# A decoder trunk in float32: where the moving operands of its matmuls lie within 256 bytes, how factors share tiles, and who adds the last squares

## The chip, the cores and the metric

The kernel runs on one core of a Trainium2 chip. The metric is the device time of one execution in microseconds (us); lower is better. The core has TensorE for matmuls (PE in the profile, with its weight loads under PEld), VectorE (DVE), ScalarE (ACT), GpSimd (POOL) and the DMA queues, each with an instruction stream of its own; semaphores tie them together. SBUF is the memory that the engines read, PSUM the one that matmuls write.

## The reference, cut to what matters

```python
def rms_norm(x, g):
    y = x * lax.rsqrt(jnp.mean(x * x, axis=-1, keepdims=True) + 1e-6)
    return y * g
def swiglu(x, w_gate, w_up, w_down):
    return (jax.nn.silu(x @ w_gate) * (x @ w_up)) @ w_down
for layer in range(2):                         # x: 512 tokens x 1024
    x = x + 0.5 * swiglu(rms_norm(x, ffn1_norm), ...)     # 1024 -> 2816 -> 1024
    hn = rms_norm(x, mix_norm)
    x = x + (pool_mla_mixer(hn, ...) if layer == 0 else gated_conv_mixer(hn, ...))
    x = x + 0.5 * swiglu(rms_norm(x, ffn2_norm), ...)
```

Everything is float32. There are four feed-forward blocks, one mixer with pooling and attention, one with a short gated convolution, and six norms that are taken over the 1,024 channels of a token.

## The kernel before

Tokens lie along the free dimension: `x[k]` holds 128 channels by 512 tokens, for k from 0 to 7. A matmul keeps a 128x128 block of weights stationary and streams activations as the moving operand, 512 tokens or, in the feed-forward blocks, half of them (256 columns). To reach float32 precision each product is made of three matmuls on operands that are split in a high and a low half: `whi` with the high half of the activation, `whi` with its low half, `wlo` with its high half. `split` (L86 to L88) makes such halves: ScalarE rounds the high half, VectorE subtracts.

**Feed-forward block** (`ffn`). A 2x2 block product is done with seven multiplications in place of eight, so weights and activations are combined first. The seven combinations of the normed input are the tiles `fB11`, `fT1`, `fN2`, `fB21`, `fT3`, `fN22`, `fT4` (8,192 bytes in a partition, the high halves in the first 4,096 and the low halves behind). Eleven pairs p of hidden blocks each pass through seven gate/up products P1 to P7 (`gate_up`); a product is 24 matmuls with 256 columns, all with the one line L461. The result h of a pair is again split into seven factors (`blocks`, `pair_halves`), which the down products read (`down`): four pairs in the first group, four in the second, three in the last, so 24 or 18 matmuls to a product. In all four blocks together 6,720 gate/up and 3,696 down matmuls have 256 columns. `staggered` sets the order of the products of neighbouring units, and `weights()` the order of loads and splits. Four quarters of weights are loaded for each unit, and combinations of them are made by DMAs that add to what lies in SBUF.

Around the feed-forward blocks 1,668 matmuls of the three-fold kind have 512 columns: on the scaled input `xh`, `xl` (1,200), the convolution's `vh`, `vl` (192), the mixer's `mh`, `ml` and some of attention.

**Places of tiles.** Pools lay their tiles one behind the other in each partition, so a tile's address is settled by what stands ahead of it. Every weight half starts at 128 bytes past a multiple of 256. Read off the built programs, the start of a moving operand past a multiple of 256 bytes is:

| moving operand | columns | matmuls | before | after the change |
|---|---|---|---|---|
| `fB11` to `fT4` (gate/up) | 256 | 6,720 | 160 | 64 |
| factors of h in the pool `hy` (down) | 256 | 2,064 | 160 | 64 |
| factors of h in the pool `hx` (down) | 256 | 1,632 | 128 | 64 |
| `xh`, `xl` | 512 | 1,200 | 128 | 128 |
| `vh`, `vl` (convolution) | 512 | 192 | 0 | 128 |
| `mh`, `ml` (mixer) | 512 | 204 | 64 | 128 |
| attention, and its projections | 256 to 512 | 360 | 64 | 128 |

Before, a factor's two 256-column blocks share one 2,048-byte tile and the low halves lie in another tile of the pools `hx` or `hy`, at whatever distance these give; `slot` picks the pool by p.

**Norms.** `squares` has ScalarE square `x[k]`; GpSimd adds the squares of k = 0 to 5 into `acc` (L250), and those of 6 and 7 are kept in `Norm.late`. `norm_columns` sums over channels with small matmuls (`ones` as moving operand, two columns): 4 blocks of tokens for each of the three tiles, and as they are plain float32, two passes for each, so 24. VectorE and ScalarE make the reciprocal root, `norm_rows` spreads it over the partitions (L333), and ScalarE copies it to the tile `R` (L335), which the whole normed input waits for (`normal`). `copied` (L466) puts the sums `x1` and `x2` of P1, P7 and P6 in SBUF.

Of the kernel before, what the change touches and what calls it, by code (L numbers as in the profile page):

```python
# [10 lines left out]
F32 = mybir.dt.float32  # L11
F32R = mybir.dt.float32r
# [4 lines left out]
P = 128  # L17
D = 1024
T = 512
FF = 2816  # L20
NK = D // P
NF = FF // P
NT = T // P
# [12 lines left out]
HT = T // 2  # L36
# [5 lines left out]
def trunk(ctx: ExitStack, tc: tile.TileContext, a, out):  # L42
# [12 lines left out]
    nc = tc.nc  # L55
    const = ctx.enter_context(tc.tile_pool(name="const", bufs=1))
    xp = ctx.enter_context(tc.tile_pool(name="xp", bufs=1))
    wp = ctx.enter_context(tc.tile_pool(name="wp", bufs=3))
    hx = ctx.enter_context(tc.tile_pool(name="hx", bufs=16))
    tp = ctx.enter_context(tc.tile_pool(name="tp", bufs=2))  # L60
    sp = ctx.enter_context(tc.tile_pool(name="sp", bufs=3))
    pp = ctx.enter_context(tc.tile_pool(name="pp", bufs=6, space=bass.MemoryType.PSUM))

    def bank(tag="bank", bufs=None):
# [10 lines left out]
    ones = const.tile([P, 2], F32, name="ones")  # L75
# [10 lines left out]
    def split(raw, hi, lo):  # L86
        nc.scalar.copy(hi, raw)  # L87
        nc.vector.tensor_sub(lo, raw, hi.bitcast(F32))  # L88
# [75 lines left out]
    for l in range(2):  # L164
        for f in ("ffn1", "ffn2"):
# [21 lines left out]
            for kind, p in what:  # L187
                if kind == "gu":
                    units.append(seven([gu[p, q] for q in range(4)], CH, turn))
                else:  # L190
                    gi, e = p
# [35 lines left out]
    xs = [None] * NK  # L227

    class Norm:
        acc = None  # L230
        late = []

    def scaled(k, which):
        g = gains[:, which, k:k + 1]
        xh = hx.tile([P, T], F32R, tag="hx", name=f"xh{k}")
        xl = hx.tile([P, T], F32R, tag="hx", name=f"xl{k}")
        nc.scalar.activation(xh, x[k], AF.Copy, scale=g)
        nc.vector.scalar_tensor_tensor(xl, x[k], g, xh.bitcast(F32), ALU.mult, ALU.subtract)  # L238
        xs[k] = (xh, xl)
# [69 lines left out]
    def token_sums(ps, acc):  # L309

        for i in range(NT):
            nc.tensor.matmul(ps[:, 2 * i:2 * i + 2], acc[:, i * P:(i + 1) * P], ones,
                             start=True, stop=True)

    def norm_columns():

        ps = held()
        parts = [Norm.acc, *Norm.late]
        Norm.late.clear()
        for j, acc in enumerate(parts):  # L320
            for i in range(NT):
                nc.tensor.matmul(ps[:, 2 * i:2 * i + 2], acc[:, i * P:(i + 1) * P], ones,  # L322
                                 start=i + j == 0, stop=j == len(parts) - 1, skip_group_check=True)
        v = sp.tile([P, NT], F32, tag="nv", name="nv")
        nc.vector.tensor_scalar(v, ps[:, 0:2 * NT:2], 1.0 / D, EPS, ALU.mult, ALU.add)
        return rsqrt(v, NT, "n")
# [12 lines left out]
    def ffn(l, f, which, after, first=False):  # L339
        what, order = plans[l, f]  # L340
        with ExitStack() as es:
# [59 lines left out]
            quarter(banks[0:2], 4, False, True)  # L401
            quarter(banks[2:4], 4, False, True)

            hy = es.enter_context(tc.tile_pool(name="hy", bufs=19, reuse_waits="tile"))
            hfac = {}

            def slot(p, i, name):
                pool = (hx if i >= 5 else hy, hx, hx, hy, hy)[p % 5]
                return pool.tile([P, T], F32R, tag="hx" if pool is hx else "hy", name=name)

            def pair_halves(p, i, src):
                hi, lo = slot(p, i, "hh"), slot(p, i + 1, "hl")
                h3, l3 = (t.rearrange("p (e t) -> p e t", t=HT) for t in (hi, lo))
                split(src, h3, l3)
                return [(hi[:, e * HT:(e + 1) * HT], lo[:, e * HT:(e + 1) * HT]) for e in range(2)]

            B12, N22, B11, T1, N2, T3, B21, T4 = range(8)

            def blocks(p, hz, rest):

                d = hfac.setdefault(p, {})
                if not rest:
                    nc.vector.tensor_sub(hz[:, T1], hz[:, B12], hz[:, B11])
                    nc.vector.tensor_add(hz[:, N2], hz[:, T1], hz[:, N22])
                    nc.vector.scalar_tensor_tensor(hz[:, T3], hz[:, N22], -1.0, hz[:, B12], ALU.mult, ALU.subtract)
                    d["B11"], d["T1"] = pair_halves(p, 0, hz[:, B11:T1 + 1])
                    d["N2"], d["T3"] = pair_halves(p, 2, hz[:, N2:T3 + 1])
                    n22 = slot(p, 4, "hn")
                    split(hz[:, N22], n22[:, :HT], n22[:, HT:])
                    d["N22"] = n22[:, :HT], n22[:, HT:]  # L430
                else:
                    nc.vector.scalar_tensor_tensor(hz[:, T4], hz[:, N2], -1.0, hz[:, B21], ALU.mult, ALU.subtract)
                    d["B21"], d["T4"] = pair_halves(p, 5, hz[:, B21:T4 + 1])


            hz = eight()
# [25 lines left out]
                                         stop=last and i == 2, skip_group_check=True)  # L462

            def copied(ps, name):
                c = fp.tile([P, T], F32, tag=name, name=name)
                nc.scalar.copy(c, ps)  # L466
                return c

# [81 lines left out]
    def even_mixer(after):  # L550
        with ExitStack() as es:
            mp = es.enter_context(tc.tile_pool(name="mp", bufs=1))

            def one(shape, name, dt=F32):
                return mp.tile(shape, dt, tag=name, name=name)
# [1 line left out]
            pcol = one([P, 4], "pcol")  # L557
            lcol = one([P, 5], "lcol")
            qcol = one([DQK, 2], "qcol")
            rcnt = one([P, 16], "rcnt")  # L560
            mask = one([P, P], "mask")
            nc.scalar.dma_start(out=pcol, in_=a["a_pool_scale"])
            nc.scalar.dma_start(out=lcol, in_=a["a_lat_gain"])
# [354 lines left out]

    def odd_mixer(after):
        with tc.tile_pool(name="op", bufs=1) as op:  # L920
            cw = op.tile([P, 3, NK], F32, tag="cw", name="cw")
            nc.scalar.dma_start(out=cw, in_=a["c_conv_w"])
            vs = []
            for j in range(NK):
                gc = bank()
                column(gc, weights(), xs)
                if j == 0:
                    r = norm_columns()
                hh = bank()
                column(hh, weights(), xs)  # L930
                if j == 0:
                    R, _ = norm_rows(r)
                    R2 = op.tile([P, T], F32, tag="Rh", name="R2", bufs=1)
                    nc.vector.tensor_mul(R2, R, R)
                gb = bank()
                column(gb, weights(), xs)
                u = tp.tile([P, T], F32, tag="t", name="u")
                nc.vector.tensor_mul(u, gc, R2)
                nc.vector.tensor_mul(u, hh, u)
                y = op.tile([P, T], F32, tag="hf", name="y", bufs=2)  # L940
                nc.vector.tensor_scalar(y, u, cw[:, 2, j:j + 1], None, ALU.mult)
                for s in (1, 2):
                    nc.vector.scalar_tensor_tensor(y[:, s:], u[:, :T - s], cw[:, 2 - s, j:j + 1], y[:, s:],
                                                   ALU.mult, ALU.add)
                b = tp.tile([P, T], F32, tag="sq", name="b")
                nc.vector.tensor_mul(b, gb, R)
                nc.vector.tensor_mul(b, b, y)
                vh = op.tile([P, T], F32R, tag=f"vh{j}", name=f"vh{j}")
                vl = op.tile([P, T], F32R, tag=f"vl{j}", name=f"vl{j}")
                split(b, vh, vl)  # L950
                vs.append((vh, vl))
            for m in range(NK):
                y = bank()
                column(y, weights(), vs)
                nc.vector.tensor_add(x[m], x[m], y)
                after(m)
# [78 lines left out]
```

## Time and profile before

| | |
|---|---|
| median of 3 runs | 1809.54 us (1809.44 to 1812.14) |
| profiled execution | 1814.28 us, of which the span of instructions is 1812.5 us |
| TensorE's mean granted clock | 0.977 of 2.4 GHz |
| busy share: PE, PEld, DVE, ACT, POOL | 96%, 91%, 73%, 50%, 17% |
| idle time of PE put down to a wait, all lines | 58.7 us |
| read from HBM | 299.06 MB |

The span is what lies between the first and the last instruction; 1.78 us of the profiled time lie outside it. Matmuls are pipelined: their durations in the trace overlap, so the rate of a stream is read from the starts of its matmuls, not from the duration of one.

### The profile page before, as it was taken

Reading aid. Unit: us, or ns where it says so; the run is one execution under the profiler, and the core shown is the slowest. Engines: PE = TensorE matmul, PEld = TensorE weight load, DVE = VectorE, ACT = ScalarE, POOL = GpSimd, SP = SyncE. Lnnn points to the kernel's source line nnn. Section 1 sums busy time; section 2 is a strip of 40 time slices with the busy share of each in tenths; the row PEclk is TensorE's granted clock in tenths of the full one; section 3 lists DMA queues with packets and bytes.
Section 4 is the critical chain, followed back from the end, with each engine's and each line's share of the span. In section 5 each row is a group of like instructions: output and inputs, shape, how many; then the busy total and the mean of one; then the engine's idle time right before and its main releaser. Section 6 shows DMA issues by size and latency. Waiting matters only on the chain.

```text
span 1812.5 us, 31505 instructions
## 1 busy us (share of the span) xinstructions
PE 1749.0 (96%) x12738; PEld 1646.9 (91%) x12738; DVE 1326.1 (73%) x1903; ACT 907.7 (50%) x1324; POOL 308.8 (17%) x359
## 2 busy tenths in 40 slices
PE   8899999999999899999989999998999999999998
PEld 6899999988888899999979999998888879999998
DVE  6877786767887877786787867867555667867866
ACT  5554554554655554554555645544322346545553
POOL 2111111124202111111111111112000201111111
PEclk8899999999999899999998999999999989999999
DMA  6689988641015689988757988885322348888985
GB/s 200 152 208 211 220 204 205 149 137 35 18 48 163 153 209 209 213 210 205 150 153 174 212 219 210 204 211 121 105 93 95 103 128 186 219 209 205 211 207 127
DMA packets 89186, 303.21 MB, mean 167 GB/s; under 512 B 10704, under 2 KB 11472, under 8 KB 89040
## 3 DMA queue, kind: packets, MB, share of 16 engines
q0 software_dynamic: 36864, 130.04, 41.1%
q1 hardware_dynamic: 50512, 169.89, 26.9%
q8 instruction: 100, 1.64, 0.4%
q10 hardware_dynamic: 1664, 1.26, 0.2%
q14 instruction: 46, 0.38, 0.1%
HBM read 299.06 MB, written 2.10 MB: 166 GB/s over the span
## 4 chain that ended last, share of the span: by engine, by line
PE 86%; DVE 6%; DMA 3%; issue 2%; ACT 2%; POOL 1%; SPq 0%; ACTq 0%; DVEq 0%; POOLq 0%
PE bank L461 63%; PE bank L215 6%; PE bank L216 6%; PE bank L217 6%; DMA sto<-in_ffn_w_down 2%; DVE wlo L88 1%; DMA sto<-in_ffn_w_gu 1%; PE held L322 1%; ACT whi L87 1%; DVE x L531 1%; DVE xn L373 1%; DVE xl L238 1%; PE bank L866 0%; PE held L215 0%; PE held L216 0%
## 5 line engine op out<-in xcount | busy, mean ns | idle before, releaser
L461 PE MATMUL bank<-fT,whi 128*128 128x256 f32 x1920 | 349.9, 283 | 0.0
L87 ACT CAST whi<-sto 128x1024 fp32r<-128x1024 f32 (+1 forms) x192 | 196.7, 1024 | 288.7 <-PE bank L461 167.1
L461 PE MATMUL bank<-hh,whi 128*128 128x256 f32 x1056 | 299.6, 284 | 9.8 <-ACT whi L87 7.8
L461 PEld LDWEIGHTS bank<-fT,whi 128*128 128x128 f32 x1920 | 299.7, 192 | 0.8 <-ACT x L466 0.8
L461 PE MATMUL bank<-hl,whi 128*128 128x256 f32 x1056 | 297.2, 282 | 1.8 <-DVE hl L88 1.8
L88 DVE TENSOR_TENSOR wlo<-sto,whi 128x1024 fp32r<-128x1024 f32 (+1 forms) x192 | 228.6, 1191 | 93.6 <-ACT whi L87 93.0
L461 PE MATMUL bank<-hh,wlo 128*128 128x256 f32 x1056 | 296.7, 282 | 0.0
L461 PE MATMUL bank<-fT,wlo 128*128 128x256 f32 x960 | 273.2, 285 | 16.5 <-DVE wlo L88 16.5
L461 PE MATMUL bank<-fN,whi 128*128 128x256 f32 x1280 | 239.7, 288 | 9.1 <-ACT whi L87 8.9
L461 PE MATMUL bank<-fB,whi 128*128 128x256 f32 x1280 | 232.8, 280 | 0.0
L461 PEld LDWEIGHTS bank<-fN,whi 128*128 128x128 f32 x1280 | 201.2, 194 | 17.0 <-ACT whi L87 10.0
L461 PEld LDWEIGHTS bank<-hh,whi 128*128 128x128 f32 x1056 | 199.8, 189 | 13.9 <-ACT whi L87 10.2
L87 ACT CAST whi<-a 128x1024 fp32r<-128x1024 f32 (+1 forms) x128 | 130.9, 1023 | 155.7 <-issue 96.8
L461 PEld LDWEIGHTS bank<-hl,whi 128*128 128x128 f32 x1056 | 200.8, 190 | 2.6 <-DVE hl L88 2.6
L461 PEld LDWEIGHTS bank<-fT,wlo 128*128 128x128 f32 x960 | 184.6, 192 | 17.3 <-DVE wlo L88 17.3
L461 PEld LDWEIGHTS bank<-hh,wlo 128*128 128x128 f32 x1056 | 199.8, 189 | 0.0
L88 DVE TENSOR_TENSOR wlo<-a,whi 128x1024 fp32r<-128x1024 f32 (+1 forms) x128 | 154.9, 1210 | 60.7 <-ACT whi L87 60.6
L461 PEld LDWEIGHTS bank<-fB,whi 128*128 128x128 f32 x1280 | 197.8, 189 | 0.3
L124 POOL DMA_DIRECT2D sto<-in_ffn_w_gu x120 | 104.7, 873 | 519.2 <-DVE wlo L88 320.4
L88 DVE TENSOR_TENSOR wlo<-ar,whi 128x1024 fp32r<-128x1024 f32 (+1 forms) x128 | 152.1, 1188 | 53.8 <-ACT whi L87 53.8
L87 ACT CAST whi<-ar 128x1024 fp32r<-128x1024 f32 (+1 forms) x128 | 130.9, 1023 | 113.7 <-PE bank L461 53.1
L461 PE MATMUL bank<-fN,wlo 128*128 128x256 f32 x640 | 183.1, 286 | 2.5 <-DVE wlo L88 2.5
(251 smaller groups left out, 3447.3 us busy)
## 6 DMA issues: line engine op xcount, KB each, us to landing
sto<-in_ffn_w_gu POOLq DMA_DIRECT2D x120, 512.0 KB, 7.1
a<-in_ffn_w_gu SPq DMA_DIRECT2D x80, 512.0 KB, 6.2
sto<-in_ffn_w_down POOLq DMA_DIRECT2D x48, 512.0 KB, 7.4
ar<-in_ffn_w_gu SPq DMA_DIRECT2D x40, 512.0 KB, 4.5
sto<-in_ffn_w_gu SPq DMA_DIRECT2D x40, 512.0 KB, 4.7
ar<-in_ffn_w_gu POOLq DMA_DIRECT2D x40, 512.0 KB, 5.4
a<-in_ffn_w_down SPq DMA_DIRECT2D x32, 512.0 KB, 5.8
raw<-in_c_w_in SPq DMA_DIRECT2D x24, 512.0 KB, 3.5
```

What stands on the lines that cost most here:

```text
L87: nc.scalar.copy(hi, raw)
L88: nc.vector.tensor_sub(lo, raw, hi.bitcast(F32))
L124: nc.gpsimd.dma_start(out=self.unit[tag], in_=self.srcs[q], accum_op=ALU.add)
L215: nc.tensor.matmul(ps, wh, ah, start=start, stop=False)
L216: nc.tensor.matmul(ps, wh, al, start=False, stop=False)
L217: nc.tensor.matmul(ps, wl, ah, start=False, stop=stop)
L238: nc.vector.scalar_tensor_tensor(xl, x[k], g, xh.bitcast(F32), ALU.mult, ALU.subtract)
L322: nc.tensor.matmul(ps[:, 2 * i:2 * i + 2], acc[:, i * P:(i + 1) * P], ones, start=i + j == 0, stop=j == len(parts) - 1, skip_group_check=True)
L373: nc.vector.scalar_tensor_tensor(xn[e][:, i], x[k], gains[:, which, k:k + 1], R if e else Rp, ALU.mult, ALU.mult)
L461: nc.tensor.matmul(o, w_[:, s], a_, start=fresh and e == 0 and k == 0 and i == 0, stop=last and i == 2, skip_group_check=True)
L531: nc.vector.scalar_tensor_tensor(o, v, 0.5 * sign, o, ALU.mult, ALU.add)
```

## The change

Padding of a few tiles, and fewer buffers in the small pool `sp`, give the starts in the last column of the table above. The factors of h now lie four to a tile: high halves of four factors in the first 4,096 bytes, low halves behind, so that high and low half of a factor are always 4,096 bytes apart, as in the tiles `fB11` to `fT4`. A table, `home`, says which factor of which pair goes where; `put` splits as many factors at a time as stand together (four, two or one). The scaled inputs `xh`, `xl` share the pool `hx` in tiles of the same size. To make room, `x1` lies in the buffer of `R`. And VectorE adds the last two squares to `acc`, so that only `acc` goes through the small matmuls.

```diff
-    hx = ctx.enter_context(tc.tile_pool(name="hx", bufs=16))
+    hx = ctx.enter_context(tc.tile_pool(name="hx", bufs=4))
-    sp = ctx.enter_context(tc.tile_pool(name="sp", bufs=3))
+    sp = ctx.enter_context(tc.tile_pool(name="sp", bufs=2))
@@ scaled
-        xh = hx.tile([P, T], F32R, tag="hx", name=f"xh{k}")
-        xl = hx.tile([P, T], F32R, tag="hx", name=f"xl{k}")
+        if k % 2 == 0:
+            Norm.tile = hx.tile([P, 4 * T + 64], F32R, tag="hx", name=f"xs{k}")
+        xh, xl = (Norm.tile[:, c * T:(c + 1) * T] for c in (k % 2, 2 + k % 2))
@@ norm_columns
-        parts = [Norm.acc, *Norm.late]
+        for sq in Norm.late:
+            nc.vector.tensor_add(Norm.acc, Norm.acc, sq)
         Norm.late.clear()
-        for j, acc in enumerate(parts):
-            for i in range(NT):
-                nc.tensor.matmul(ps[:, 2 * i:2 * i + 2], acc[:, i * P:(i + 1) * P], ones,
-                                 start=i + j == 0, stop=j == len(parts) - 1, skip_group_check=True)
+        token_sums(ps, Norm.acc)
@@ ffn
-            hy = es.enter_context(tc.tile_pool(name="hy", bufs=19, reuse_waits="tile"))
+            hy = es.enter_context(tc.tile_pool(name="hy", bufs=5))
+            home = ({"B11": (0, 0), "N2": (0, 2), "N22": (1, 0), "B21": (1, 2)},
+                    {"N22": (1, 1), "B11": (2, 0), "N2": (2, 2), "B21": (3, 0)},
+                    {"B11": (3, 2), "N2": (4, 0), "B21": (4, 2), "N22": (5, 0)},
+                    {"N22": (5, 1), "B11": (5, 2), "N2": (6, 0), "B21": (6, 2)})
+            def put(p, names, src):
+                j, c = home[p % 4][names[0]]
+                j += 7 * (p // 4)
+                if j not in four:
+                    if j in (0, 1, 2, 7, 9, 10, 14):
+                        t = hx.tile([P, 4 * T + 64], F32R, tag="hx", name="hh")[:, 48:48 + 4 * T]
+                    else:
+                        t = hy.tile([P, 4 * T], F32R, tag="hy", name="hh")
+                    four[j] = t.rearrange("p (c f t) -> p c f t", c=2, f=4)
+                v = four[j][:, :, c:c + len(names)]
+                split(src, v[:, 0], v[:, 1])
@@ blocks
-                    d["B11"], d["T1"] = pair_halves(p, 0, hz[:, B11:T1 + 1])
-                    d["N2"], d["T3"] = pair_halves(p, 2, hz[:, N2:T3 + 1])
+                    if p % 4 < 2:
+                        put(p, ("B11", "T1", "N2", "T3"), hz[:, B11:T3 + 1])
+                    else:
+                        put(p, ("B11", "T1"), hz[:, B11:T1 + 1])
+                        put(p, ("N2", "T3"), hz[:, N2:T3 + 1])
@@ copied
-                c = fp.tile([P, T], F32, tag=name, name=name)
+                c = tp.tile([P, T], F32, tag="R", name=name, bufs=1) if name == "x1" else \
+                    fp.tile([P, T], F32, tag=name, name=name)
@@ even_mixer, odd_mixer
-            rcnt = one([P, 16], "rcnt")
+            rcnt = one([P, 56], "rcnt")[:, :16]
-            cw = op.tile([P, 3, NK], F32, tag="cw", name="cw")
+            cw = op.tile([P, 10, NK], F32, tag="cw", name="cw")[:, :3]
```

What it moves in the streams shows at two places. The first is VectorE ahead of the fourth norm, the one between the two layers (`x` the residual, `xl` the low half of the scaled input, `nv` the mean square); before:

```order
L88 TENSOR_TENSOR wlo<-raw,whi 128x1024
L238 SCALAR_TENSOR_TENSOR xl_10436<-x,gains,xh_10435 128x512
L238 SCALAR_TENSOR_TENSOR xl_10442<-x,gains,xh_10441 128x512
L325 TENSOR_SCALAR nv<-held 128x4
L88 TENSOR_TENSOR wlo<-raw,whi 128x1024
```

and now:

```order
L88 TENSOR_TENSOR wlo<-raw,whi 128x1024
L319 TENSOR_TENSOR acc<-acc,sq 128x512
L239 SCALAR_TENSOR_TENSOR xs_10234<-x,gains,xs_10234 128x512 x2
L319 TENSOR_TENSOR acc<-acc,sq 128x512
L323 TENSOR_SCALAR nv<-held 128x4
L88 TENSOR_TENSOR wlo<-raw,whi 128x1024
```

The two additions stand on either side of the last two low halves, so the second is the last thing ahead of `nv`. The fifth norm has the same order; in the first norm an addition stands behind each of the last two low halves, and in the other three the additions stand ahead of the last low half.

On TensorE the sums of the same norm stood between two columns of the first quarter of weights (`held` is their PSUM tile):

```order
L216 MATMUL bank<-xl_10290,whi 128x512
L217 MATMUL bank<-xh_10289,wlo 128x512
L322 MATMUL held<-ones,acc 128x2 x4
L322 MATMUL held<-ones,sq 128x2 x8
L215 MATMUL bank<-xh_10268,whi 128x512
```

and now stand two matmuls further on, a third as many:

```order
L215 MATMUL bank<-xs_10076,whi 128x512
L216 MATMUL bank<-xs_10076,whi 128x512
L313 MATMUL held<-ones,acc 128x2 x4
L217 MATMUL bank<-xs_10076,wlo 128x512
L215 MATMUL bank<-xs_10076,whi 128x512
```

The second place is ScalarE at the start of the feed-forward block behind the mixer of layer 0, where the first `x1` is copied; before (`t` is the gate of the first pair, `sto` and `a` are weights):

```order
L466 COPY x_6659<-bank 128x512
L87 CAST fT_6415<-hz 128x1024
L441 ACT_TABLE_LOAD
L441 ACTIVATE t<-t 128x512
L87 CAST whi<-sto 128x1024
L441 ACTIVATE t<-t 128x512
L87 CAST whi<-a_6548 128x1024
```

and now:

```order
L87 CAST fT_6298<-hz 128x1024
L448 ACT_TABLE_LOAD
L448 ACTIVATE t<-t 128x512
L87 CAST whi<-sto 128x1024
L448 ACTIVATE t<-t 128x512
L474 COPY x_6536<-bank 128x512
L87 CAST whi<-a_6425 128x1024
```

The copy has moved behind a weight cast and both gates, because its tile is `R`'s buffer and VectorE still multiplies by `R` until then. The order of the feed-forward products on TensorE is the same as before.

## Rows read from the trace of the kernel before

**Rows 1.** The page, part 1: busy time, share of the span, instructions

```profile
PE 1749.0 (96%) x12738; PEld 1646.9 (91%) x12738; DVE 1326.1 (73%) x1903; ACT 907.7 (50%) x1324; POOL 308.8 (17%) x359
```

**Rows 2.** The chain in order of time (start, us, what): one unit; a late load; a norm

```profile
93.83 19.87 PE bank L461 x168
...
882.41 4.80 DMA sto<-in_ffn_w_down
...
1279.33 3.18 PE held L322 x24
```

**Rows 3.** Timeline, PE: gate/up products, first matmul, and the 96th behind it

```profile
82.34 0.40 PE L461 MATMUL bank<-fN,whi 128*128 128x256 f32 x2
...
93.54 0.28 PE L461 MATMUL bank<-fB,whi 128*128 128x256 f32 x1
```

**Rows 4.** Timeline, PE: down products, first matmul, and the 216th behind it

```profile
264.50 0.28 PE L461 MATMUL bank<-hh,whi 128*128 128x256 f32 x1
...
290.21 0.40 PE L461 MATMUL bank<-fT,whi 128*128 128x256 f32 x2
```

**Rows 5.** Timeline, PE, 512 columns: two rows each of xl, vh, mh

```profile
1292.12 0.40 PE L216 MATMUL bank<-xl,whi 128*128 128x512 f32 x1
...
1411.13 0.39 PE L216 MATMUL bank<-xl,whi 128*128 128x512 f32 x1
...
1411.59 0.40 PE L215 MATMUL bank<-vh,whi 128*128 128x512 f32 x1
...
1455.91 0.40 PE L216 MATMUL bank<-vl,whi 128*128 128x512 f32 x1
...
545.26 0.39 PE L217 MATMUL bank<-mh,wlo 128*128 128x512 f32 x1
...
563.69 0.39 PE L216 MATMUL bank<-ml,whi 128*128 128x512 f32 x1
```

**Rows 6.** Timeline, PE: the small matmuls of the first and the fourth norm

```profile
18.59 1.87 PE L322 MATMUL held<-ones,acc 128*128 128x2 f32 x8 [4.28 <-POOL acc L250]
20.32 3.55 PE L322 MATMUL held<-ones,sq 128*128 128x2 f32 x16
23.73 0.77 PE L215 MATMUL bank<-xh,whi 128*128 128x512 f32 x1
...
923.06 1.93 PE L322 MATMUL held<-ones,sq 128*128 128x2 f32 x16
924.85 0.49 PE L215 MATMUL bank<-xh,whi 128*128 128x512 f32 x1
```

**Rows 7.** Timeline, DVE: low halves ahead of norms 4 and 5; a 512-column product

```profile
921.53 1.40 DVE L238 SCALAR_TENSOR_TENSOR xl<-x,gains,xh 128x512 fp32r<-128x512 f32 x2
...
1277.58 1.40 DVE L238 SCALAR_TENSOR_TENSOR xl<-x,gains,xh 128x512 fp32r<-128x512 f32 x2
...
1293.19 0.69 DVE L934 TENSOR_TENSOR R<-R 128x512 f32<-128x512 f32 x1
```

**Rows 8.** Windows behind norms 4 to 6: busy by engine, PEclk, DMA share, GB/s

```profile
924.85:929.60 4.75, 4.75 (x16) 3.75 (x16) 2.48 (x8) 0.20 (x1) 0.08 (x1) 0.64 0.98 197
1282.30:1287.70 5.40, 5.40 (x14) 4.24 (x15) 2.65 (x8) 2.53 (x3) 0.00 (x0) 0.50 0.18 44
...
1464.40:1468.90 4.50, 4.50 (x15) 3.54 (x15) 2.48 (x8) 0.21 (x1) 0.86 (x1) 0.62 1.02 207
```

**Rows 9.** Timeline at a block's start: the copy of x1; ScalarE's gate; PE

```profile
592.59 0.58 ACT L466 COPY x<-bank 128x512 f32<-128x512 f32 x1 [0.48 <-PE bank L461]
...
603.88 0.62 ACT L441 ACTIVATE t<-t 128x512 f32<-128x512 f32 x1
...
605.29 0.58 PE L461 MATMUL bank<-fN,wlo 128*128 128x256 f32 x1 [0.76 <-DVE wlo L88]
```

**Rows 10.** Windows in gate/up products and in down products, columns as in 8

```profile
199.17:217.15 17.98, 17.96 (x154) 17.76 (x153) 13.89 (x21) 11.28 (x17) 3.50 (x4) 1.00 0.88 216
142.07:167.79 25.72, 25.72 (x219) 25.72 (x218) 19.27 (x24) 10.57 (x12) 3.56 (x5) 1.00 0.92 225
```

More of the change, by code (lines that the diff above doesn't have):

```diff
@@ L402, in ffn @@
             quarter(banks[2:4], 4, False, True)
-            hy = es.enter_context(tc.tile_pool(name="hy", bufs=19, reuse_waits="tile"))
[L405 to L415, printed above, removed]
+            hy = es.enter_context(tc.tile_pool(name="hy", bufs=5))
+            hfac, four = {}, {}
+            home = ({"B11": (0, 0), "N2": (0, 2), "N22": (1, 0), "B21": (1, 2)},
[3 rows of a table added]
+            def put(p, names, src):
[9 more added lines that the diff above has]
+                split(src, v[:, 0], v[:, 1])
+                hfac.setdefault(p, {}).update({b: (v[:, 0, i], v[:, 1, i]) for i, b in enumerate(names)})
             B12, N22, B11, T1, N2, T3, B21, T4 = range(8)
             def blocks(p, hz, rest):
-                d = hfac.setdefault(p, {})
                 if not rest:
@@ L425, in blocks @@
                     nc.vector.scalar_tensor_tensor(hz[:, T3], hz[:, N22], -1.0, hz[:, B12], ALU.mult, ALU.subtract)
-                    d["B11"], d["T1"] = pair_halves(p, 0, hz[:, B11:T1 + 1])
-                    d["N2"], d["T3"] = pair_halves(p, 2, hz[:, N2:T3 + 1])
-                    n22 = slot(p, 4, "hn")
-                    split(hz[:, N22], n22[:, :HT], n22[:, HT:])
-                    d["N22"] = n22[:, :HT], n22[:, HT:]
+                    if p % 4 < 2:
[3 more added lines that the diff above has]
+                        put(p, ("N2", "T3"), hz[:, N2:T3 + 1])
+                    put(p, ("N22",), hz[:, N22:N22 + 1])
                 else:
                     nc.vector.scalar_tensor_tensor(hz[:, T4], hz[:, N2], -1.0, hz[:, B21], ALU.mult, ALU.subtract)
-                    d["B21"], d["T4"] = pair_halves(p, 5, hz[:, B21:T4 + 1])
+                    put(p, ("B21", "T4"), hz[:, B21:T4 + 1])
             hz = eight()
```

## The prediction

> **What bounds the kernel.** I read the page first: TensorE is busy for 96% of the span [rows 1]. Then the chain of work that ended last, in order of time: a gate/up unit of 168 matmuls stands in it as one piece of 19.87 us [rows 2]. So the kernel goes as fast as its matmuls start, and what counts is the time from start to start, here 118.3 ns for each matmul of 256 columns, with one short stop in it. The timeline gives undisturbed rates at the different places of the moving operand:
>
> - 256 columns, start at 160: 11.20 us for 96 matmuls, 116.7 ns [rows 3].
> - 256 columns, down products whose factors lie partly at 128 and partly at 160: 25.71 us for 216, 119.0 ns [rows 4].
> - 512 columns at 128: 119.01 us for 525, 226.7 ns; at 0: 44.32 us for 190, 233.3 ns; at 64: 18.43 us for 79, 233.3 ns [rows 5].
>
> The reader is to see that matmuls of one shape on one engine differ by 2% to 3% with nothing waiting, and that the place within 256 bytes goes with it. It need not be the cause: the down products also have halves at all distances. The loads are not the bound while this goes on, but they are near: 0.88 and 0.92 of the DMA engines' time [rows 10].
>
> **The 256-column streams.** All 10,416 now start at 64, with halves 4,096 bytes apart. No row shows 256 columns at 64 against weights at 128, so the price has two bounds. From below: in 512 columns at 128 a matmul takes 226.7 ns, so 113.3 ns for each 256 columns, the best rate in any row. From above: 512 columns at 64 cost 233.3 - 226.7 = 6.6 ns a matmul more than at 128; if that is a price of each matmul whatever its length, 256 columns at 64 take 119.0 + 6.6 = 125.6 ns. Between them lie 116.7 (no effect of the place, beyond no more mixing) and 119.0 (as the down products now).
>
> I take 114 ns, near the lower end. The levels in the rows look like steps for each 256 columns: 113.3 (512 at 128) and 116.7 (256 at 160, and 512 at 0 and 64, each half of 233.3). If so the place decides between the two, and what is good depends on the length: 128 bytes are one sixteenth of an operand of 2,048 bytes, and 64 are one sixteenth of one of 1,024. That is a guess from three places, no more; 0.7 ns are kept for streams that fall out of step after a stop.
>
> Gate/up: of 6,720 matmuls about 6,400 run undisturbed, at 117.0 ns on average (116.7 in most units; 118.3 less its stop in rows 2 is 117.2). (117.0 - 114) x 6,400 = 19.2 us saved. Down, first two groups: 7 x 4 x 4 products of 24, so 2,688 matmuls, (119.0 - 114) x 2,688 = 13.4 us. The third group's 1,008 matmuls I count at nothing: there the chain runs through loads, such as the 4.80 us in rows 2, and a faster matmul waits longer. Together 32.6 us. Against that, the down stretches would ask for 5 in 119 more of DMA engines that are at 0.92 already, 0.96 [rows 10]; I give back 3 us for loads that come late.
>
> **The 512-column streams.** `vh`, `vl` and most of `mh`, `ml` stand in streams that wait for nothing: (192 + 192) x 6.6 ns = 2.5 us saved, as they move to the place of `xh`.
>
> **The norms.** Each norm loses 16 small passes. In the fourth they take 1.79 us, in the first, at a lower clock, 3.41 us [rows 6]; 3.41 + 5 x 1.79 = 12.4 us saved. In their place VectorE makes two additions of 512 columns, some 0.65 us each behind one another by the nearest row, 0.69 us for a product of that size [rows 7]. Where these end late, TensorE stands waiting, for the sums are now behind them. First norm: the first addition waits for GpSimd's last one, which freed TensorE at 18.59 [rows 6]; addition, the last low half (0.7 to 0.9 us), addition end near 20.8, 2.2 us later than now. Fourth norm: the two low halves run from 921.53 for 1.40 us [rows 7], so with both additions VectorE is done at about 924.2, and TensorE is at the sums about 922.5 (16 passes from 923.06 now, 8 ahead of them at half that time, two matmuls more ahead): 1.8 us. Fifth: 1277.58 + 1.40 + 1.3 = 1280.3 [rows 7] against a start at 1279.33 [rows 2]: 1.0 us. In the other three VectorE is done in time. What is queued behind an addition is the next `wlo` and `nv`, which waits for the sums anyway. So 5.0 us are given back, 7.4 stay.
>
> Behind norms 4, 5 and 6 the granted clock falls to 0.64, 0.50 and 0.62 over some 5 us, that is TensorE at the 1.2 GHz level for most of it [rows 8]. It costs 4.75 x 0.36 + 5.40 x 0.50 + 4.50 x 0.38 = 6.1 us. It follows a stretch of passes with two columns each, which becomes a third as long; but in norms 4 and 5 a wait takes its place. I count half, 3 us; the bounds are 6 saved and, if norms 2 and 3 begin to fall as well, 4 lost.
>
> **x1 in R's buffer.** The first `x1` of a block was copied at 592.59 with ScalarE idle; now it stands behind ScalarE's gate at 603.88, and ends near 605.1 [rows 9]. The bank that it reads is the one P6 adds to, so P6's first two matmuls start after the copy, some 1 us later; but its third waits for `wlo` until 605.29 in any case [rows 9]. At most 0.3 us of TensorE's work moves, in four blocks 1 us lost; without that cover it would be 4.
>
> **At nothing.** Four factors split at a time: the same elements on ScalarE and VectorE in fewer instructions. VectorE is at 13.89 of 17.98 us in a gate/up stretch [rows 10], and the last pair of a block, which down products follow at once, is still split by twos. Coarser tiles, fewer `sp` buffers: a tile is asked for again some 20 us or a whole norm after its last use; if one came late, a group's first product would wait a split, about 1 us.
>
> **The sum**: -32.6 + 3 - 2.5 - 7.4 - 3 + 1 = -41.5 us, against the profiled execution's 1814.3 us (span 1812.5 and 1.8 outside it): 1772.8. That execution was 4.7 us above the median of the runs, 1809.5, so for the median 1809.5 - 41.5, rounded: **1768 us**.
>
> **The rivals.** *The place does nothing to 256 columns*, which then run at 116.7 to 117.0 everywhere; the down products gain by no longer mixing places: (119.0 - 116.8) x 2,688 = 5.9 us. With 2.5 + 7.4 + 3 - 1 = 11.9 from the rest that is 17.8 saved: 1792 us. For it speaks that 116.7 holds over a whole unit, as if something other than the moving operand set it. Against it, that the 512-column streams do change with nothing but the place. In the Trainium skill, "TensorE: Matmul & The Clock Gate", section "Back-to-back issue gap", the gap at full clock depends on the number of columns alone; the 226.7 and 233.3 ns here differ at one number of columns, and both lie over its 215.8 (109.2 for 256, by the same formula, against 116.7). By that rule the time would be this rival's without the 512-column streams' gain, 1794 us.
>
> *64 is as 128 was*: all 256-column streams at 119.0. Gate/up loses 2.0 x 6,400 = 12.8 us, down gains nothing, the rest saves 11.9: 1810.4 us, no change that can be told. For it speaks that the down products, the only 256-column ones not all at 160, are the slow ones.
>
> *The price of 64 seen with 512 columns holds for each matmul*, 125.6 ns: gate/up loses 8.6 x 6,400 = 55.0, down 6.6 x 2,688 = 17.7 us, the rest saves 11.9: 1870 us, slower. It decides from 118.9 ns a matmul on; below that the kernel is faster, since (118.9 - 117.0) x 6,400 = 12.2 us is what the rest saves. For it speaks the one row at 64.
>
> **Chances and range.** 114 ns or near (113.3 to 115.5), 1768 us with 1756 to 1785 of its own: 0.42. No effect, 1785 to 1800: 0.26. As at 128, 1800 to 1822: 0.20, of which faster 0.04, within 0.2% 0.10, slower 0.06. As with 512 columns, or between, above 1822: 0.12. A measurement of this kernel tells about 0.2%, 3.6 us, from no change. Faster: 0.42 + 0.26 + 0.04 = 0.72; same 0.10; slower 0.18. The range, 1757 to 1819, leaves out a bit of the first case, some of the third and all of the fourth.
>
> **What would show it.** In the profile after: 96 gate/up matmuls in 10.9 us (11.2 if the place does nothing, 11.4 as at 128, 12.0 at the worst), the down products at the same rate, `vh` at 227 ns; 8 passes at each norm with waits for VectorE's additions in norms 1, 4 and 5; a granted clock of 1.00 behind norm 6. The prediction is wrong above all if 64 is no good place for 256 columns, and in part if the loads, at 0.92, do not keep up.

## The result, and the profile after

The changed kernel takes 1788.1 us (median of 4 runs, 1784.1 to 1791.0) against 1809.5 us before (1807.6 to 1812.1): a ratio of 0.988, 95% interval 0.985 to 0.991. The forecast was 1768 us, in a range of 1757 to 1819. The profiled execution took 1785.9 us (span 1784.1), 28.4 us less than that of before; it lies 2.2 us below its median, that of before 4.8 us above.

Page of after, part 1 [rows 1]:

```profile
PE 1704.7 (96%) x12642; PEld 1601.1 (90%) x12642; DVE 1329.4 (75%) x1891; ACT 907.0 (51%) x1300; POOL 310.4 (17%) x359
```

Timeline of after, PE, in pairs (the first matmul of a stretch without a stop, and one a counted number behind it): gate/up, 72 apart; down, 456 apart; gate/up at another place, 72 apart; `vh`, 183 apart (it answers to [rows 3 to 5]):

```profile
101.49 0.39 PE L468 MATMUL bank<-fB,whi 128*128 128x256 f32 x2
...
109.65 0.28 PE L468 MATMUL bank<-fB,whi 128*128 128x256 f32 x1
...
135.06 0.39 PE L468 MATMUL bank<-fT,whi 128*128 128x256 f32 x2
...
186.74 0.28 PE L468 MATMUL bank<-fB,whi 128*128 128x256 f32 x1
...
81.39 0.40 PE L468 MATMUL bank<-fB,whi 128*128 128x256 f32 x2
...
89.87 0.28 PE L468 MATMUL bank<-fB,whi 128*128 128x256 f32 x1
...
1387.59 0.39 PE L215 MATMUL bank<-vh,whi 128*128 128x512 f32 x1
...
1429.07 0.39 PE L215 MATMUL bank<-vh,whi 128*128 128x512 f32 x1
```

Gate/up: 8.16 us / 72 = 113.3 ns. Down: 51.68 / 456 = 113.3 ns. But the third pair gives 8.48 / 72 = 117.8 ns, with operands at the same place within 256 bytes as in the first. So 256 columns at 64 have two levels, at a granted clock of 1.00 both times. `vh` takes 41.48 / 183 = 226.7 ns.

The chain in order of time shows what stands between the streams now:

```profile
69.75 0.03 DVEq L88
69.79 0.26 DVE c L511
70.05 0.04 issue
70.09 8.33 PE bank L468 x71
78.43 0.04 issue
78.46 19.35 PE bank L468 x163
97.82 0.30 ACT hh L87
98.12 0.49 ACT x L474
98.61 0.04 issue
98.65 11.18 PE bank L468 x96
```

Where a unit was one piece of 168 matmuls [rows 2], the chain leaves TensorE at 69.75 for VectorE's difference `c` and at 97.82 for ScalarE: a split of factors, then the copy of x1. Over the whole span, the waits of PE (us in total, times, longest):

```profile
PE bank L468 <- DVE wlo L88: 22.5, 13, 4.2
PE bank L468 <- ACT x L474: 15.8, 12, 4.1
PE bank L468 <- ACT whi L87: 11.0, 13, 1.5
PE held L313 <- DVE acc L319: 8.9, 3, 6.7
```

The second is new: `x L474` is the copy of x1. Most of its time lies at the starts of blocks, where a load is late as well: at each of the four starts the high half of P6's weights was ready only 1.0 us before the copy ended.

The norms: small passes of norms 1, 3 and 4, and the windows behind norms 4 to 6 (columns as in [rows 8]):

```profile
19.26 1.87 PE L313 MATMUL held<-ones,acc 128*128 128x2 f32 x8 [6.74 <-DVE acc L319]
...
561.37 0.80 PE L313 MATMUL held<-ones,acc 128*128 128x2 f32 x6 [0.77 <-DVE acc L319]
...
911.87 1.05 PE L313 MATMUL held<-ones,acc 128*128 128x2 f32 x8 [1.35 <-DVE acc L319]
```

```profile
912.80:916.33 3.53, 3.53 (x17) 2.89 (x17) 2.48 (x8) 0.21 (x1) 0.28 (x1) 1.00 0.97 217
1261.91:1267.01 5.10, 5.10 (x25) 4.22 (x25) 2.56 (x8) 1.64 (x4) 0.00 (x0) 1.00 0.32 103
1437.36:1440.90 3.54, 3.54 (x17) 2.90 (x17) 2.47 (x8) 0.42 (x2) 1.47 (x2) 1.00 1.03 312
```

Eight passes in place of 24, waits for VectorE's additions in norms 1, 3 and 4, and a granted clock of 1.00 where it was 0.64, 0.50 and 0.62.

I made an account from the starts of all matmuls in both traces, each feed-forward block cut at its first P6 product (`fN2`) and at the end of its last P7 gate/up product (`fT3`). (Of the eleven pairs of a block ten pass through the seven gate/up products, which gives the 6,720 matmuls; the first pair is made from the scaled input.)

| us, profiled executions | before | after | |
|---|---|---|---|
| first products of the 4 blocks | 58.1 | 61.2 | +3.1 |
| 9,024 matmuls in the middle: streams | | | -31.0 |
| the same: stops over 130 ns | 27.0 | 35.2 | +8.3 |
| ends of the 4 blocks | 165.2 | 171.5 | +6.3 |
| between the blocks (norms, mixers) | 496.7 | 481.8 | -14.9 |

That is -28.2 of the 28.4 us. In the middle the undisturbed matmuls (up to 130 ns from start to start) take 117.6 ns before and 114.0 after. The new stops there are two: `fB11` to `fN22`, where P3 waits for `c`, 4.5 us before and 7.8 after (28 times), and `fT4` to `fN2`, where P6 waits for x1's copy, none before and 5.2 us after (25 times). The second matmul behind such a stop comes some 0.11 us late as well, 68 times in place of 40; shorter waits elsewhere make up for that.

Two rows of the account also hold a low clock. In the end of each of the four blocks the granted clock is 0.50, the 1.2 GHz level, for a stretch (windows of after, columns as in [rows 8]):

```profile
337.80:341.20 3.40, 3.40 (x18) 3.40 (x18) 2.22 (x4) 0.63 (x1) 0.88 (x1) 0.50 0.66 136
877.10:880.50 3.40, 3.40 (x18) 3.40 (x17) 2.69 (x4) 0.83 (x1) 0.43 (x1) 0.50 0.77 154
1225.30:1228.60 3.30, 3.01 (x14) 3.01 (x15) 2.57 (x4) 0.11 (x1) 0.88 (x1) 0.50 0.37 62
1750.90:1754.30 3.40, 3.40 (x18) 3.40 (x17) 2.37 (x5) 0.83 (x1) 0.80 (x1) 0.50 0.60 136
```

TensorE had waited for weights just ahead (0.82 and 0.75 us in the first block). Before, only the first block's end has such a stretch. Counted by the starts of the matmuls, this costs 5.9 us after and 1.5 before, so 4.4 of the 6.3 us at the ends are the clock. The stops of the middle hold 8.0 us of this kind after and 7.8 before, behind the late loads at the blocks' starts.

### The profile page after: what moved, and what is told of

It reads as the page before. It is cut to its first block, busy times and chain, and to the rows that moved or that the text cites. A ratio compares the mean times of both kernels' runs of the same rounds, so it can differ in the third digit from the quotient of the medians.

```text
span 1784.1 us, 31312 instructions
## 1 busy us (share of the span) xinstructions
PE 1704.7 (96%) x12642; PEld 1601.1 (90%) x12642; DVE 1329.4 (75%) x1891; ACT 907.0 (51%) x1300; POOL 310.4 (17%) x359
## 4 chain that ended last, share of the span: by engine, by line
PE 80%; DVE 10%; issue 4%; ACT 3%; DMA 2%; POOL 1%; SPq 0%; ACTq 0%; DVEq 0%; POOLq 0%
PE bank L468 62%; PE bank L216 5%; PE bank L215 5%; PE bank L217 5%; DVE wlo L88 2%; ACT whi L87 1%; DMA sto<-in_ffn_w_gu 1%; DVE xn L371 1%; DVE xs L239 1%; DMA sto<-in_ffn_w_down 1%; DVE x L539 1%; DVE fT L88 1%; DVE fB L88 1%; PE bank L874 0%; PE held L215 0%
## 5 line engine op out<-in xcount | busy, mean ns | idle before, releaser
L468 PE MATMUL bank<-hh,whi 128*128 128x256 f32 x2464 | 434.3, 280 | 15.2 <-ACT whi L87 11.0
L468 PEld LDWEIGHTS bank<-hh,whi 128*128 128x128 f32 x2464 | 377.4, 190 | 19.7 <-ACT whi L87 13.6
L468 PE MATMUL bank<-hh,wlo 128*128 128x256 f32 x1232 | 344.3, 280 | 7.0 <-DVE wlo L88 7.0
L468 PE MATMUL bank<-fT,whi 128*128 128x256 f32 x1920 | 341.2, 281 | 0.4 <-ACT x L474 0.4
L468 PEld LDWEIGHTS bank<-fT,whi 128*128 128x128 f32 x1920 | 296.1, 192 | 1.3 <-ACT x L474 1.3
L468 PEld LDWEIGHTS bank<-hh,wlo 128*128 128x128 f32 x1232 | 234.4, 191 | 8.9 <-DVE wlo L88 8.9
L468 PE MATMUL bank<-fB,whi 128*128 128x256 f32 x1280 | 228.2, 277 | 0.0
L88 DVE TENSOR_TENSOR wlo<-ar,whi 128x1024 fp32r<-128x1024 f32 (+1 forms) x128 | 152.3, 1190 | 48.3 <-ACT whi L87 48.2
L468 PE MATMUL bank<-fB,wlo 128*128 128x256 f32 x640 | 177.4, 277 | 0.0
L216 PE MATMUL bank<-xs,whi 128*128 128x512 f32 x392 | 155.0, 395 | 2.5 <-DVE xs L239 2.3
```

The source lines that it names most:

```text
L216: nc.tensor.matmul(ps, wh, al, start=False, stop=False)
L468: nc.tensor.matmul(o, w_[:, s], a_, start=fresh and e == 0 and k == 0 and i == 0, stop=last and i == 2, skip_group_check=True)
```

## The experiments

My theory after this: the place gives the stream 113.3 ns, and most of what the prediction missed is taken back by fixed chains on ScalarE and VectorE inside a block and by late loads at its ends. Rivals: the new layout gives the rate, not the place; the loads take everything back; the clock stays up for another reason. The ratios stand against runs of the kernel before on the same chip.

**The place, undone.** `place160`: the changed kernel, operands at 160.

```diff
             fp = es.enter_context(tc.tile_pool(name="fp", bufs=1))
+            fp.tile([P, 24], F32, tag="pad", name="pad")
-   ... name="hh")[:, 48:48 + 4 * T]
+   ... name="hh")[:, 8:8 + 4 * T]
```

> The changed kernel, with the 256-column moving operands of the feed-forward blocks back at 160 past a multiple of 256 (a pad of 96 bytes ahead of them, and the offset in the hx tiles); halves still 4,096 bytes apart, four factors to a tile. If the place sets the rate: 116.7 to 117.8 ns a matmul in gate/up and down in place of 113.3, some 3.3 ns for 9,000 matmuls, 29 us, less some 5 us of waits for ScalarE's copy that the slower stream hides again: about 1812 us against 1788 of the changed kernel. If the equal distance of the halves gives it, whatever the place: 113.3 ns still, 1788 us.

1799.4 us, ratio 0.994 (0.992 to 0.996). Timeline, PE, gate/up, 72 apart:

```profile
79.40 0.40 PE L469 MATMUL bank<-fB,whi 128*128 128x256 f32 x2
...
87.80 0.28 PE L469 MATMUL bank<-fB,whi 128*128 128x256 f32 x1
```

8.40 / 72 = 116.7 ns; other stretches run at 117.8; down runs at the same two levels, no longer at 118.9 to 119.5. So it is not the equal distance of the halves that gives 113.3. 64 against 160 is worth 11 us, not the 24 I had expected: in the profiled executions the streams of the middle lose 25 us, but 12 come back in shorter stops (6.1), ends (4.7) and starts (1.3).

**The place alone.** `before64`: the kernel before, with a pad of 160 bytes, the same line with `[P, 40]`.

> The kernel before, with one pad of 160 bytes ahead of the pool of the block: gate/up operands and the factors in hy start at 64, the factors in hx stay at 128; nothing else is changed. If the place alone sets the rate: gate/up at 113.3 ns a matmul, 6,400 x 3.4 = 22 us saved less some 4 of waits for the fixed chains of ScalarE and VectorE: about 1791 us against 1809.5; the down products show what mixed distances and two places give. If the new layout of factors gives it: gate/up stays at 116.7 ns, 1809 us.

1799.5 us, ratio 0.993 (0.991 to 0.996). Gate/up, 96 matmuls apart:

```profile
100.66 0.39 PE L462 MATMUL bank<-fN,whi 128*128 128x256 f32 x2
...
111.54 0.28 PE L462 MATMUL bank<-fB,whi 128*128 128x256 f32 x1
```

10.88 / 96 = 113.3 ns, with nothing changed but the place. Only some 60% of gate/up runs so, the rest at 117.8: that, and `fB11` to `fN22` (6.8 us in place of 4.5), is why 12 us came and not 18. Down mixes operands at 64 and at 128 in the first two groups and runs at 115.9 to 118.4 there; in the third, whose factors lie nearly all in `hy`, stretches at 113.3 to 114.4 and at 117.8 appear.

**The norms, undone.** `oldnorms`: the changed kernel with `norm_columns` of before (three tiles, 24 passes).

> The changed kernel with the norms of before (24 passes, no additions on VectorE). If the passes bring the clock down behind norms 4 to 6: granted clock 0.5 to 0.65 there again, and between the feed-forward blocks some 12 us more (all but the 1.3 us of vh and vl), about 1800 us. If the clock stays up for another reason (the streams ahead of the norms run at another rate now): only passes less waits, some 5 to 7 us, about 1794 us, with a granted clock near 1.00.

1797.9 us, ratio 0.993 (0.991 to 0.996): 9.8 us more than the change; between the blocks 493.2 us against 481.8. Windows behind norms 2 and 5:

```profile
377.72:383.29 5.57, 5.57 (x14) 4.41 (x15) 4.71 (x12) 2.57 (x4) 0.32 (x1) 0.50 0.21 72
1270.50:1274.50 4.00, 4.00 (x13) 3.17 (x13) 2.15 (x7) 2.53 (x3) 0.00 (x0) 0.57 0.07 12
```

The clock falls again, but behind norms 2 and 5, and not behind 4 and 6. So 24 passes do bring it down, but which norms are hit varies: over norms 2 to 6, 9 of 15 in the three traces with 24 passes (before, `before64`, this one). With 8 passes it is 8 of 55 in eleven traces, seven of them behind norm 4, where TensorE has just stood idle for 0.9 to 1.4 us for the additions (in the other four traces it stood there for 0.8 to 1.4 us and the clock stayed up). The changed kernel's own trace has none: part of its gain is luck, some 1 us by these counts (an estimate).

**x1's copy.** `x1first`: a priority puts it ahead of the splits on ScalarE.

```diff
                 if s == "P1":
-                    u["x1"] = copied(ps, "x1")
+                    with tc.high_priority(60):
+                        u["x1"] = copied(ps, "x1")
```

> The changed kernel with one line more: the copy of x1 gets a higher priority, so that it stands ahead of the splits of factors on ScalarE. If that queue is what stops the faster stream: the 25 waits between fT4 and fN2 (5.2 us in all) are gone, and some of the stretches at 117.8 ns that begin behind them, 2 to 4 us: about 1780 us against 1788. If the loads set the pace there: the wait shows up at another weight, 1788 us.

1786.2 us (1784.2 to 1794.2), ratio 0.986 (0.984 to 0.988). ScalarE at the same place, the changed kernel and then `x1first`:

```profile
95.72 1.06 ACT L87 CAST whi<-a 128x1024 fp32r<-128x1024 f32 x1 [1.24 <-issue]
96.68 1.44 ACT L87 CAST hh<-hz 128x512 fp32r<-128x512 f32 x3
98.03 0.57 ACT L474 COPY x<-bank 128x512 f32<-128x512 f32 x1
```

```profile
95.83 1.06 ACT L87 CAST whi<-a 128x1024 fp32r<-128x1024 f32 x1 [1.34 <-issue]
96.79 0.58 ACT L474 COPY x<-bank 128x512 f32<-128x512 f32 x1
97.26 1.45 ACT L87 CAST hh<-hz 128x512 fp32r<-128x512 f32 x3
```

All 25 waits are gone, and the stops in the middle fell from 35.2 to 25.3 us. But the time hardly moved, and the profiled execution (its longest, 1794.2 us) shows why for itself: 69% of its undisturbed 256-column matmuls ran at 117.8 ns, against 17% in that of the changed kernel, and the streams of the middle took 21 us more. In the traces a stream keeps its level until a stop: with fewer stops it stays longer where it is, at the good level or the bad. That this also held the other three executions back is not shown, for they have no trace.

The rows above are of a pair split by twos. In the changed kernel there are 28 places of this kind: at 12 the copy stands behind one cast of four factors (2.4 us of waits in all), at 8 behind three smaller casts (2.6 us), and at 8 behind two (0.2 us). So the bigger pieces are half of it at most; what in the change moved the copy behind the smaller ones is not shown.

**Fewer loads.** `fewloads`: `add` issues nothing.

> The changed kernel without the loads that GpSimd issues to add a second block of weights onto a first; the products then run on uncombined weights. If the loads are what the faster streams run into at both ends of a feed-forward block: the last 43 us of each block fall towards 36, the start from 15.3 to 13 or less, 30 us or more in all, about 1755 us, while the waits at fB11 behind fN22 and at fN2 behind fT4 (13 us) stay, for they come from ScalarE and VectorE. If ScalarE and VectorE are the bound at the ends too: 1785 us.

1743.4 us in one run. The window over the end of the first block, the changed kernel and then `fewloads`:

```profile
322.70:365.58 42.88, 38.37 (x301) 36.97 (x301) 33.66 (x47) 21.14 (x32) 11.93 (x13) 0.96 0.58 119
```

```profile
316.60:355.50 38.90, 36.64 (x301) 35.62 (x301) 33.24 (x47) 21.10 (x32) 5.87 (x6) 1.00 0.18 59
```

And what ended ScalarE's idle time ahead of the weight casts (group view, same order):

```profile
L87 ACT CAST whi<-sto 128x1024 fp32r<-128x1024 f32 (+1 forms) x192 | 196.5, 1023 | 289.8 <-PE bank L468 148.7 <-DMA sto<-in_ffn_w_gu 58.9 <-DMA sto<-in_ffn_w_down 43.2
```

```profile
L87 ACT CAST whi<-sto 128x1024 fp32r<-128x1024 f32 (+1 forms) x192 | 196.1, 1024 | 218.0 <-PE bank L468 151.3 <-issue 51.4 <-DVE wlo L88 9.1
```

The ends, with 300 matmuls each as before, fall from 171.5 to 152.3 us; the starts from 61.2 to 57.8 while each holds 18 matmuls more (the order moved), so by about 12 like for like, and the middle by about 12 as well. The two stops of the middle stay (10.9 us against 13.0). As expected, then: the ends and starts wait for loads, these two stops for ScalarE and VectorE. But with the waits for loads the low clock goes too: in middle and ends no stretch below 1.00 is left, which is 8.0 and 5.9 us of the gain. On average the loads take 0.58 of the DMA engines' time in the window of the changed kernel, so when they come may matter more than what the engines can carry; whether it is the bytes or the order in which the second load waits for the first product's casts, this run does not tell apart.

**A version without the chain.** `ycopy`: `x1first`, and Y is copied behind P5 in place of X behind P7, into the buffer that `acc` leaves free.

```diff
+                elif s == "P5":
+                    u["x3"] = copied(ps, "x3")
...
-                    x3 = copied(ps, "x1")
                     c = summed()
-                    nc.vector.tensor_sub(c, u["Y"], x3)
+                    nc.vector.tensor_sub(c, u["x3"], ps)
```

> The changed kernel with x1's copy ahead as before this, and with the other operand of one difference copied: Y behind P5 in place of X behind P7, so that P3 (fN22) no longer waits for a copy and a subtraction that start only when P7 has ended. If these fixed chains of ScalarE and VectorE are what takes back the gain inside a block: the 28 waits at fN22 (6 to 8 us) are gone, 1779 us or so against 1786 with x1's copy ahead alone. If a wait also lets a stream that has settled at 117.8 ns come back to 113.3: fewer waits, fewer chances to come back, and executions that lie further apart; then the waits are gone and the time stays within 3 us of 1786.

1767.5 us (1761.7 to 1777.5), ratio 0.977 (0.974 to 0.980): faster than both kernels, and below both figures that I had expected. Chain in order of time, the two longest pieces of the first two blocks:

```profile
103.33 209.34 PE bank L468 x1845
...
612.27 243.26 PE bank L468 x2063
```

209.34 / 1845 = 113.5 ns in the first block, 243.26 / 2063 = 117.9 in the second. The stops in the middle are down to 12.9 us, 8.4 of which are the low clock at the blocks' starts. The ends are at 161.2 us, 10 less than in the changed kernel with every load in place, of which 1.2 are the clock; what gave the rest was not tried, so the loads are not all that sets the ends. Two of the four blocks ran at 113.4 almost from end to end (259.9 and 258.8 us for the middle), two at 117.4 to 117.8 (268.0 and 268.1). So one block's level is worth 9 us, which would explain why executions lie 16 us apart (only one is traced). All four blocks at the good level would take about 1749 us (estimate: 1766.1 less 2 x 8.7).

**What the place is measured from.** Four versions of `ycopy`: weights at 192 (`w192`, pads ahead of the weights and behind them), operands at 192, 32 and 96 (the pads of `place160` in other sizes); and two of the changed kernel, operands at 128 and 0.

> The version with Y's copy, with all weight halves at 192 past a multiple of 256 in place of 128 and the moving operands where they were (256 columns at 64, xs at 128). If a moving operand's own place sets the rates: 113.3 or 117.8 ns in blocks as before, 1767 us. If the distance between the places of weights and moving operand sets them: 64 against 192 is 128 apart, as 0 against 128 is, so 118.7 to 120 ns as with operands at 0, some 1790 us; and xs at 128 against 192, as 64 against 128 was, 233.3 ns.

> The version with Y's copy, with the 256-column operands at 192, weights at 128. By the operand's own place the rows tell nothing of 192 yet: at 64, 160, 0 and 128 the best rates are 113.3, 116.7, 118.7 and 120.0 ns. If 64 on either side of the weights is alike: 113.3 or 117.8, 1767 us. If 64 is good for the single reason that it lies 64 below the weights: 116.7 ns or more, 1785 us or more.

> The version with Y's copy, 256-column operands at 32, 96 below the weights. If only the distance to the weights counts and its levels lie in order (best rates 120.0, 116.7, 113.3 and 118.7 ns at 0, 32, 64 and 128 so far): between 64 and 128, so 113.3 to 118.7, without a second level if we are lucky: 1750 us if it is 113.3 throughout, some 1790 at 118. If 32 bytes off a stretch of 64 cost the same on any side: 116.7 and 117.8 as at 160, about 1782 us.

> The version with Y's copy, 256-column operands at 96, 32 below the weights; 160 is 32 above them. If the sign of the distance does not count: 116.7 and 117.8 ns as at 160, and little difference between the two levels, so executions close together, about 1780 us against 1767. If it counts: another level.

> The changed kernel with the 256-column operands at 128, where 512 columns run at their best rate, 226.7 ns. If what is a good place goes with the length of the operand, as the prediction guessed: not 113.3 ns but 116.7 to 119 a matmul, about 1805 us. If one place is good for all lengths: 113.3 ns, about 1788 us. If a stream may settle at one of two rates, as the runs before this one show at 64 (113.3 and 117.8): 117.8 in part of its stretches here as well.

> The changed kernel with the 256-column operands at 0, where 512 columns take 233.3 ns. If a place is as good for 256 columns as it is for 512: 116.7 ns at best, about 1800 us. If 64 and 0 are alike for 256 columns (both at the start of a stretch of 64 bytes, which 160 is not): 113.3 ns at best, about 1788 us.

`w192` takes 1797.0 us, ratio 0.991 (0.989 to 0.993). Its timeline, 240 gate/up matmuls apart, and 346 of 512 columns on `xs`:

```profile
70.09 0.40 PE L471 MATMUL bank<-fN,whi 128*128 128x256 f32 x2
...
98.57 0.40 PE L471 MATMUL bank<-fN,whi 128*128 128x256 f32 x2
...
1299.79 0.39 PE L220 MATMUL bank<-xs,wlo 128*128 128x512 f32 x1
...
1380.52 0.39 PE L218 MATMUL bank<-xs,whi 128*128 128x512 f32 x1
```

28.48 / 240 = 118.7 ns and 80.73 / 346 = 233.3 ns: the operands have not moved, the weights have, and the levels are those of an operand 128 and 64 away from the weights. So in both cases tried the distance modulo 256 between moving operand and weights counts, and not the operand's own place. The levels in stretches without a stop (`place` versions are of the changed kernel, `w192` and those with y of `ycopy`, so their times are compared only within a kind):

| operand less weights | columns | ns a matmul | seen in | us, median |
|---|---|---|---|---|
| -96 (32 against 128) | 256 | 117.1 to 117.5, 118.4 to 118.9 | `y32` | 1785.4 |
| -64 (64 against 128) | 256 | 113.3, 117.8 | after, `ycopy` | 1788.1, 1767.5 |
| -32 (96 against 128) | 256 | 118.0 to 118.7 | `y96` | 1786.5 |
| 0 (128 against 128) | 256 | 120.0 | `place128` | 1822.9, one run |
| +32 (160 against 128) | 256 | 116.7, 117.8 | `place160` | 1799.4 |
| +64 (192 against 128) | 256 | 113.3, 117.8 | `y192` | 1786.6 |
| 128 (0/128, 64/192) | 256 | 118.4 to 119.1, some 120 | `place0`, `w192` | 1815.7 (one run), 1797.0 |
| 0 | 512 | 226.7 | `xs`, `vh` after | |
| -64, 128 | 512 | 233.3 | `mh`, `vh` before, `xs` in `w192` | |

`place128` and `place0` are slower than any of their expectations (120.0 ns against 116.7 to 119, and 118.4 to 119.1 against 116.7 at best). `y96` fell outside its first expectation: 32 below the weights is not 32 above them. `y192` has both levels of 64, but ran at 117.8 in nearly all of its profiled execution, and its four runs (1782.8 to 1789.0) lie near the 1784 that four blocks at 117.8 would give. `y32` is not between 113.3 and 118.7 throughout; it has two levels near 117 and 119, and no place tried holds 113.3 alone.

## Why the prediction came out as it did

The range and the side were right; the point was 20 us too low. 1788.1 lies outside the 1756 to 1785 that the prediction gave its own case, in the band that it gave to no effect of the place: that the whole range held is owed to the rivals in it. Of the 20 us, 13 are in the terms below, and the rest lies in the two profiled executions, 4.8 us above and 2.2 below their medians.

- **256-column streams, -32.6:** -31.0 in the middle of the blocks. 114 ns was right as a mean (114.0), by luck, and not as a level: 113.3 in most stretches and 117.8 in the others. The allowance of 0.7 ns "for streams that fall out of step after a stop" is the second level, 4.4 ns dearer. The guess behind it (an operand's place in steps of its length) fell: the place counts from the weights.
- **The third group's 1,008 at nothing:** right; the ends of the blocks gained nothing (+6.3, of which 4.4 are the clock), and `fewloads` shows that loads hold them up.
- **Loads, +3, and x1, +1:** the step that failed, in size and partly in cause. These were all that the blocks were to give back, 4 us; measured are 17.7 (8.3 + 3.1 + 6.3), 4.4 of them for a clock that the prediction looked for at the norms alone. The loads did not come late where the term put them: at 113.3 ns the down stretch from 135.06 ran 51.68 us without a stop at a DMA share of 0.92. What came late inside the blocks was ScalarE and VectorE. P3's wait for the chain copy, difference, product takes a fixed time, so that a shorter stream ahead of it becomes a longer wait (+3.3 us).
- **"At nothing: four factors split at a time":** wrong in part. The splits take no longer in sum, but x1's copy, which stood behind the first of them (0.6 us), stands behind up to 1.44 us of casts now: +5.2 us. About half of it comes behind a cast of four factors, the rest behind smaller ones, so the order did it as much as the pieces. I had looked for x1's delay only at a block's start; there the cover held.
- **Norms, -7.4, and clock, -3, 512 columns, -2.5:** 12.9 forecast, 14.9 measured. The additions' waits came in norms 1 and 4, not in 5, and in norm 3, where I had seen none. The clock gave back 5.8 of its 6.1 us in this execution (matmul by matmul behind norms 4, 5 and 6: 1.6, 2.6 and 1.6), where I had counted half; `vh`, `vl`, `mh` and `ml` gave 1.8, and 7.3 are left for passes and waits. By `oldnorms` it is not the same norms in each execution.
- **The rivals:** 1792, *the place does nothing*, is the nearest in time and wrong in mechanism: `before64` shows 113.3 with only the place changed. *As at 128* would have been 120.0, by `place128`.

## What to carry to other kernels

When a stream of matmuls waits for nothing, take its time from start to start and compare stretches: one shape at one granted clock can have several levels, set by where moving operand and weights lie against each other, and a pad of some bytes moves it. Before you count the gain of a faster stream, list the fixed chains that it runs into (here copy, subtraction, product) and see in the instruction order what the change puts ahead of each link, for equal work in another order or in coarser pieces is not equal work for what queues behind it. Look at the granted clock behind each wait too, not only where you expect it low: here the ends of the blocks lost more to it than to longer waits. And where a stream can settle at two levels, judge a version by several executions, since one profile can show either.

## What the runs showed of the hardware

- Two levels at one place, 113.3 and 117.8 ns, kept over 2,000 matmuls and changed only at stops or within a dozen matmuls behind one. What picks the level is open. In the traces of the changed kernel, `oldnorms` and `x1first`, after a stream at 113.3 had stopped between `fB11` and `fN22`, a stop of 375 to 376 ns led back to 113.3 in 26 of 26 cases, one of 372 to 373 ns to 117.8 in 6 of 6, and one of 374 ns to either: the next level goes with a few nanoseconds of the stop, which need not be what causes it. At other stops, of about 311 or 456 ns, both levels follow.
- In the Trainium skill, "TensorE: Matmul & The Clock Gate", section "Back-to-back issue gap", the formula for the gap of an isolated matmul at full clock has the number of columns alone in it. The streams here, with a weight load for each matmul, differ by 6% at 256 columns (113.3 to 120.0 ns) and by 3% at 512 (226.7 and 233.3 ns) with the shape unchanged.
- The best distance from the weights is not the same for both lengths: 0 is the best of those seen for 512 columns and the worst for 256.
